# One comparison a chunk pair with a product in its other arm; 1/rms and gates inside the selections; the last scatter prepared ahead of the last products

## The chip, the core and the metric

The kernel runs on one core of a Trainium2 chip. Time is device time in microseconds, the median of three runs. The profile is of one further execution of the same program. TensorE (PE in the rows, PEld its weight loads) multiplies matrices, VectorE (DVE), ScalarE (ACT) and GpSimd (POOL) work on elements, SyncE's queue (SPq) issues the transfers from the chip's memory.

## The reference

A decoder trunk of two layers over 256 tokens of 1024 channels, float32. The change lies in the second half of layer 1, an expert layer that sends each token to two of eight experts, and in the final norm:

```python
def moe_swiglu(h, router_w, wg, wu, wd):          # h: RMS-normed, D = 1024
    logits = (t @ router_w).astype(jnp.float32)
    top_val, top_idx = lax.top_k(logits, TOP_K)   # 2 of 8
    gates = jax.nn.softmax(top_val, axis=-1)
    combine = jnp.sum(jax.nn.one_hot(top_idx, N_EXPERTS, dtype=jnp.float32) * gates[..., None], axis=1)
    for e in range(N_EXPERTS):                    # EXPERT_DIM = 3584
        he = jax.nn.silu(t @ wg[e]) * (t @ wu[e])
        out = out + (combine[:, e:e + 1].astype(t.dtype) * he) @ wd[e]
```

Around it, `h = h + moe_swiglu(rms_norm(h, ln_ffn_odd), ...)` and at the end `rms_norm(h, final_g)`. Ahead of it stand layer 0 (attention, a recurrent block, a dense SwiGLU) and the pooling mixer of layer 1; the change leaves them as they are.

## The kernel before

The order of the instructions on each engine is written out by hand; semaphores between engines are set by the framework.

**Routing.** Behind the pooling mixer `h` is complete (`band_out`, L819). It is transposed into `hT` (L844 to L850), multiplied with the router weights (`logits`, L830), and VectorE ranks the eight logits of each token (L858 to L864). Three small products give each token its slot in each expert's list (L866 to L870; `pos` L895, `cnt` L896: how many tokens an expert has). Short products on constants (`keep_warm`, L89) run in between. The squares of `h` (`squares`, L239, on ScalarE) and the nine steps of 1/rms (`finish_rs`, L223 to L243, on VectorE) come beside and behind this. Two banks of results, `go` and `yo`, are set to zero by products with a zeroed tile (L914 to L916).

**Slots.** An expert has room for 96 slots, 64 main ones (C0) and 32 more (C1). `gather_a` (L929) compares slot numbers with `pos` and so makes the selection, four comparisons an expert; `gather_b` (L939) multiplies `h` with it and `gather_c` (L944) applies the norm's gain and stores the expert's tokens in `xe`. Four small products (`slot_scales`, L955) give each slot its 1/rms and its gate; a copy (L957) keeps them.

**Chunks.** Each of the 8 experts is cut into 7 chunks of 512 hidden channels, 56 in all. A chunk has four gate/up pieces and two down pieces of 1 MB, loaded on SyncE's queue in the order: gate/up of chunk n, then down of chunk n-1. The stage has about twenty buffers for them, reused in a fixed turn; a buffer's next load is issued when the products that read it are done (`finished`, `load_free`, L144). Per chunk, TensorE does: `gate_up_main` (L971), 64 slots, two products side by side; then, only where the expert has more than 64 tokens, `gate_up_more` (L983), 32 products of 32 columns, four side by side, inside a branch (L978); ScalarE and VectorE then form silu(gate) x up with the slot scales (`hidden_a`, L990 and L991), while TensorE does `down_main` of the chunk before (L1008) and, in a second branch (L1014), its `down_more` (L1019, 8 products); last, three transposes (L997) whose result ScalarE copies (L999) for the next chunk's down products. A branch is TensorE's alone: its sequencer compares a register that holds whether the expert is full. In a full expert both branches run their products, in a small one they are skipped.

Jobs between the quarters of `gate_up_main` are listed by chunk and quarter (`do(n, q, ...)`, run by `due`): the next expert's selection and gather in the last four chunks of an expert, its slot scales in the last one, and the finished expert's scatter in the next expert's second and third chunk: `scatter_a` (L1031, L1032) transposes the selection, `scatter_b` (L1041) multiplies it with the results that `results` copied from `y` and `yo` (L1023, L1024), `scatter_c` (L1049) adds onto `ho`.

**End.** Behind the last chunk come, in this order, the last down products, `results`, `scatter_a`, and twice `scatter_b` with `scatter_c`; then `norm_out`: the final gains are spread over the partitions by four products (L1068) and copied (L1069), squares of `ho` (L239), the nine steps, four scalings (L1156) and four output transfers (L1157). A block for experts with more than 96 tokens stands behind a branch at the end and is not run with these inputs.

Of the kernel before, what the change touches and what calls it, by code (L numbers as in the profile page):

```python
# [18 lines left out]
P = 128  # L19
S = 256  # L20
# [37 lines left out]
def hybrid_kernel(ctx, tc, x, cst, prm, row, gate, rtr, w_in, w_out, w_gu, w_dn, w_pool, m_gu, m_dn, out):  # L58
# [613 lines left out]
    sc2 = late.tile([P, NT, E, 2], F32, name="sc2")  # L672
# [168 lines left out]
    for t in range(NT):  # L841
        band_out(t, 0)
    tb = [transpose_pair(kk) for kk in range(2)]
# [6 lines left out]
    dve.tensor_copy(hT[:, 6:8, :], tb[1])  # L850
    lgb = bank("tp", "lg")
# [4 lines left out]
    squares(0)  # L856
# [17 lines left out]
    squares(1)  # L874
# [34 lines left out]
    sel, xe, scl, het, y_ = {}, {}, {}, {}, {}  # L909
    yt = late.tile([P, W], F32, tag="band", name="yt")  # L910
    ysb, selT = yt[:, 0:1024].rearrange("p (a c) -> p a c", a=2), yt[:, 1024:1536].rearrange("p (a s) -> p a s", a=2)

    go, yo = bank2("go", "go"), bank2("yo", "yo")
    pool.memset(ysb, 0.0)  # L914
    for b in (go, yo):
        pe.matmul(b, ysb[:, 0, 0:P], ysb[:, 0], start=True, stop=True)  # L916

    def counted():
        dve.tensor_reduce(gt[:, 2, 0:1], cnt, axis=AX.X, op=OP.max)
        dve.tensor_copy(most, gt[:, 2, 0:1])  # L920
# [26 lines left out]
    def each_slot(s_):  # L947
        return s_.rearrange("p t m s -> p t (m s)")[:, :, P - C0:P + C1]
# [16 lines left out]
    def gate_up_main(n, b, i):  # L965

        x_ = xe[n // EP % 2]
        for kk in range(2):
            for c in range(2):
                k = 2 * i + kk  # L970
                pe.matmul(b[c * C0:(c + 1) * C0], x_[:, k, 0:C0], block(MOE[n] + i, (2 * kk + c) * 512), start=k == 0, stop=k == KD - 1)  # L971
# [3 lines left out]
    def gate_up_more(n):  # L975

        x_ = xe[n // EP % 2]
        with tc.If(big[n // EP] > 0, preferred_fallthrough_block=True):  # L978
            for k in range(KD):
                for c in range(2):  # L980
                    for r in range(2):
                        q = (2 * c + r) * C1
                        pe.matmul(go[q:q + C1, 0:2 * P], x_[:, k, C0:CAP], block(MOE[n] + k // 2, (k % 2 * 2 + c) * 512 + r * 2 * P, 2 * P),  # L983
                                  start=k == 0, stop=k == KD - 1)
# [344 lines left out]
```

## Time and profile before

| | us |
|---|---|
| median of three runs | 1201.91 (1201.18 to 1203.38) |
| the profiled execution | 1200.26 |
| its span, first to last instruction | 1198.5 |
| TensorE busy in the span | 1144.6 (96%) |
| VectorE, ScalarE, GpSimd busy | 300.1, 255.1, 99.5 |
| mean granted clock of TensorE | 0.988 |

The span is that of the profiled execution alone, so sums from its rows are made against 1200.26. A row of the timeline begins with the start in us from the span's first instruction and the time of the merged instructions; in square brackets stands the idle time ahead of it and what ended it. PEq is TensorE's sequencer. A product in float32 is recorded as two instructions, and the ends of products are modelled, so products that follow each other overlap in the rows: the time from one to the next is read from their starts.

### The profile page before, as it was taken

How to read it: one execution, taken by the hardware profiler on the slowest of the kernel's cores; microseconds unless marked ns; L12 is line 12 of the kernel's file. 1: busy time of each engine (PE TensorE's matmuls, PEld its weight loads, DVE VectorE, ACT ScalarE, POOL GpSimd, SP SyncE). 2: the span in 40 equal slices, each digit the busy share in tenths (PEclk: the TensorE clock that was granted, in tenths of full speed). 3: DMA queues.
4: the chain of work that ended last, by engine and by line, in shares of the span. 5: the costliest groups of instructions: out<-in, count | busy, mean ns of one | idle time of the engine just before them, and what ended most of it. 6: DMA issues, size and time to landing. Idle time of an engine off the chain costs nothing. (4 is left out here: it accounts for less than half of the span.)

```text
span 1198.5 us, 17142 instructions
## 1 busy us (share of the span) xinstructions
PE 1144.6 (96%) x7098; PEld 593.3 (50%) x7099; DVE 300.1 (25%) x566; ACT 255.1 (21%) x489; POOL 99.5 (8%) x115
## 2 busy tenths in 40 slices
PE   7989999999999999998989999999999999999994
PEld 6877999999843433332323443333334333443331
DVE  6686665455720011011001000200110010001002
ACT  5855544444500010110000000100100000001011
POOL 3723151112100000000000000000000000000000
PEclk8989999999999999999999999999999999999998
DMA  9444955555599999999999999999999999999951
GB/s 350 142 141 162 363 188 181 206 177 205 214 381 415 419 415 419 415 415 418 416 419 414 417 415 414 421 401 418 415 403 416 415 419 415 380 362 390 407 222 38
DMA packets 69633, 408.70 MB, mean 341 GB/s; under 512 B 7828, under 2 KB 8088, under 8 KB 31128
## 3 DMA queue, kind: packets, MB, share of 16 engines
q1 hardware_dynamic: 69384, 407.08, 85.0%
q8 instruction: 81, 1.33, 0.4%
q10 hardware_dynamic: 144, 0.10, 0.1%
q14 instruction: 24, 0.20, 0.0%
HBM read 406.10 MB, written 1.05 MB: 340 GB/s over the span
## 5 line engine op out<-in xcount | busy, mean ns | idle before, releaser
L971 PE MATMUL mg<-raw,xe 128*64 128x512 f32 x920 | 211.2, 598 | 4.2 <-DMA raw<-in_m_gu 4.0
L991 DVE SCALAR_TENSOR_TENSOR sg<-sg,scl,mg 128x256 f32<-128x256 f32 x56 | 26.9, 480 | 396.2 <-ACT sg L990 396.2
L168 DVE TENSOR_TENSOR lo<-raw,hi 128x1024 fp32r<-128x1024 f32 x80 | 100.0, 1270 | 95.7 <-ACT hi L167 95.5
L971 PEld LDWEIGHTS mg<-raw,xe 128*64 128x64 f32 x920 | 61.2, 136 | 121.8 <-issue 104.8
L990 ACT ACTIVATE sg<-mg,scl 128x256 f32<-128x256 f32 x56 | 26.6, 475 | 439.4 <-PE mg L971 439.4
L1008 PE MATMUL y<-raw,het 128*64 128x512 f32 x440 | 101.9, 598 | 7.4 <-PEq L978 4.5
L167 ACT ACTIVATE hi<-raw 128x1024 fp32r<-128x1024 f32 x96 | 98.7, 1052 | 43.3 <-PE dn L185 28.3
L999 ACT COPY het<-tp 128x384 f32<-128x384 f32 x56 | 26.8, 479 | 232.1 <-PE tp L997 231.7
L1008 PEld LDWEIGHTS y<-raw,het 128*64 128x64 f32 x440 | 32.3, 136 | 71.1 <-issue 63.7
L1008 PE MATMUL y<-twohi,het 128*64 128x512 f32 x116 | 53.6, 598 | 3.7 <-PEq L978 3.1
L971 PE MATMUL mg<-twohi,xe 128*64 128x512 f32 x212 | 55.8, 605 | 0.0
L971 PE MATMUL mg<-twolo,xe 128*64 128x512 f32 x212 | 54.5, 592 | 0.0
L1008 PE MATMUL y<-twolo,het 128*64 128x512 f32 x116 | 53.6, 600 | 0.2 <-DMA twolo<-in_m_dn 0.2
L185 PE MATMUL gu<-xfl,hi 128*128 128x256 f32 x352 | 50.3, 283 | 0.0
L185 PE MATMUL gu<-xfh,hi 128*128 128x256 f32 x352 | 50.1, 283 | 0.0
L185 PE MATMUL gu<-xfh,lo 128*128 128x256 f32 x352 | 50.0, 283 | 0.0
L185 PEld LDWEIGHTS gu<-xfh,hi 128*128 128x128 f32 x352 | 46.3, 191 | 0.9
L185 PEld LDWEIGHTS gu<-xfl,hi 128*128 128x128 f32 x352 | 45.7, 192 | 0.2 <-DVE xfl L270 0.2
L185 PEld LDWEIGHTS gu<-xfh,lo 128*128 128x128 f32 x352 | 45.7, 192 | 0.0
L168 POOL TENSOR_TENSOR lo<-raw,hi 128x1024 fp32r<-128x1024 f32 x16 | 39.3, 2456 | 70.8 <-ACT hi L167 54.0
L997 PEld LDWEIGHTS tp<-pr,sg 128*128 128x128 f32 x168 | 17.4, 140 | 53.8 <-issue 51.7
L971 PE MATMUL mg<-spare,xe 128*64 128x512 f32 x176 | 42.0, 598 | 0.0
(384 smaller groups left out, 1410.8 us busy)
## 6 DMA issues: line engine op xcount, KB each, us to landing
raw<-in_m_gu SPq DMA_DIRECT2D x115, 1024.0 KB, 16.0
raw<-in_m_dn SPq DMA_DIRECT2D x55, 1024.0 KB, 17.3
twohi<-in_m_gu SPq DMA_DIRECT2D x53, 512.0 KB, 12.3
twolo<-in_m_gu SPq DMA_DIRECT2D x53, 512.0 KB, 12.5
raw<-in_w_gu SPq DMA_DIRECT2D x22, 1024.0 KB, 4.9
spare<-in_m_gu SPq DMA_DIRECT2D x22, 1024.0 KB, 12.3
twohi<-in_m_dn SPq DMA_DIRECT2D x29, 512.0 KB, 13.1
twolo<-in_m_dn SPq DMA_DIRECT2D x29, 512.0 KB, 12.6
```

The source lines that it names most:

```text
L167: act.activation(hi, r, AF.Copy)
L168: eng.tensor_tensor(lo, r, hi.bitcast(F32), op=OP.subtract)
L185: pe.matmul(dst, l, r, start=start, stop=stop)
L971: pe.matmul(b[c * C0:(c + 1) * C0], x_[:, k, 0:C0], block(MOE[n] + i, (2 * kk + c) * 512), start=k == 0, stop=k == KD - 1)
L990: act.activation(v_, g_[:, :, 0, :], AF.Silu, scale=s4[:, a:a + 1])
L991: dve.scalar_tensor_tensor(v_, v_, s4[:, a + 1:a + 2], g_[:, :, 1, :], op0=OP.mult, op1=OP.mult)
L997: pe.transpose(b[:, i * P:(i + 1) * P], sg[:, i, :], ident)
L999: act.copy(het[n].rearrange("p a c -> p (a c)"), b[:, 0:3 * P])
L1008: pe.matmul(y_[e][j * C0:(j + 1) * C0], het[n][:, r, c * C0:(c + 1) * C0], block(DOWN[n] + c, (2 * j + r) * 512), start=p == c == r == 0, ...
```

## The change

The square sums of `h` move up between `band_out` and the logits, and 1/rms is finished before them. The two banks are zeroed by ScalarE. The gather's selection holds 1/rms (one comparison with a multiplication for each of the two token tiles), and a second selection, made by `gates` in each expert's fourth chunk, holds the gate and is transposed for the scatter in the fifth (`scatter_a`); `slot_scales` is gone, and `hidden_a` has no scales. Per chunk there is one branch (two in an expert's first chunk, one for each expert): its arm holds `gate_up_more` of this chunk and `down_more` of the one before, and its other arm one product of one column. The second of the eight k-products of `gate_up_main` (k = 1) is put behind the branch. The scatter multiplies the second part of the slots first. The gains of the final norm are made in the last chunk's second quarter; at the end, the two halves of the last scatter have banks of their own, and the squares go token tile by token tile. The block for more than 96 tokens is adapted alike.

```diff
...
     for t in range(NT):
         band_out(t, 0)
+    squares(0)
     tb = [transpose_pair(kk) for kk in range(2)]
...
     dve.tensor_copy(hT[:, 6:8, :], tb[1])
+    squares(1)
+    finish_rs()
     lgb = bank("tp", "lg")
     logits(lgb)
...
     keep_warm(WARM[0], ones)
-    squares(0)
...
-    squares(1)
 
     def slot_scalars_a():
...
     def slot_scalars_b():
         act.activation(gt[:, 1], gt[:, 0], AF.Tanh, scale=0.5)
 
-        one8 = cs[:, C_ONE:C_ONE + E]
-        for t in range(NT):
-            dve.tensor_scalar(sc2[:, t, :, 0], one8, rs[:, t:t + 1], None, op0=OP.mult)
         for t in range(NT):
             dve.scalar_tensor_tensor(cmb[:, t, :], sgn[:, t, :], gt[:, 1, t:t + 1], mskb[:, t, :], op0=OP.mult, op1=OP.add)
-        for t in range(NT):
-            dve.tensor_scalar(sc2[:, t, :, 1], cmb[:, t, :], rs[:, t:t + 1], 0.5, op0=OP.mult, op1=OP.mult)
+        dve.tensor_scalar(cmb, cmb, 0.5, None, op0=OP.mult)
...
+    selr = late.tile([P, NT, P], F32, name="selr")
+    selg = yt[:, 1536:2048].rearrange("p (t m s) -> p t m s", t=NT, m=2)
+
     go, yo = bank2("go", "go"), bank2("yo", "yo")
-    pool.memset(ysb, 0.0)
-    for b in (go, yo):
-        pe.matmul(b, ysb[:, 0, 0:P], ysb[:, 0], start=True, stop=True)
+    act.activation(go[:, 0:2 * P], iota.rearrange("p (o s) -> p o s", o=1).to_broadcast([P, 2, P]), AF.Copy, scale=0.0)
+    act.activation(yo, iota.rearrange("p (o s) -> p o s", o=1).to_broadcast([P, 4, P]), AF.Copy, scale=0.0)
...
     def gather_a(e):
-
-        s_ = sel[e] = (yt[:, 1536:2048].rearrange("p (t m s) -> p t m s", t=NT, m=2) if e % 2 else
-                       late.tile([P, NT, 2, P], F32, tag="sel", name="sel"))
+        for t in range(NT):
+            dve.tensor_scalar(selr[:, t, 0:CAP], iota[:, 0:CAP], pos[:, t, e:e + 1], rs[:, t:t + 1], op0=OP.is_equal, op1=OP.mult)
+
+    def gates(e):
         for t in range(NT):
             for m, (a, c) in enumerate(((0, C0), (C0, C1))):
-                dve.tensor_scalar(s_[:, t, m].rearrange("p (o s) -> p o s", s=c),
+                dve.tensor_scalar(selg[:, t, m].rearrange("p (o s) -> p o s", s=c),
                                   iota[:, a:a + c].rearrange("p (o s) -> p o s", o=1).to_broadcast([P, P // c, c]),
-                                  pos[:, t, e:e + 1], None, op0=OP.is_equal)
+                                  pos[:, t, e:e + 1], cmb[:, t, e:e + 1], op0=OP.is_equal, op1=OP.mult)
...
-    def slot_scales(e):
-
-        b = misc("sl")
-        for m in range(2):
-            for t in range(NT):
-                pe.matmul(b[:, 2 * m:2 * m + 2], sel[e][:, t, m], sc2[:, t, e, :], start=t == 0, stop=t == NT - 1)
-        scl[e] = work.tile([P, 4], F32, name="scl", bufs=2)
-        dve.tensor_copy(scl[e], b[:, 0:4])
...
-    def gate_up_main(n, b, i):
+    def gate_up_main(n, b, k):
 
         x_ = xe[n // EP % 2]
-        for kk in range(2):
+        for c in range(2):
+            pe.matmul(b[c * C0:(c + 1) * C0], x_[:, k, 0:C0], block(MOE[n] + k // 2, (k % 2 * 2 + c) * 512), start=k == 0, stop=k == 1)
...
-        with tc.If(big[n // EP] > 0, preferred_fallthrough_block=True):
-            for k in range(KD):
...
+    def more(parts):
+
+        for e in sorted({n // EP for _, n in parts}):
+            with tc.If(big[e] > 0, preferred_fallthrough_block=True) as c:
+                for f, n in parts:
+                    if n // EP == e:
+                        f(n)
+            with c.Else():
+                pe.matmul(go[0:C1, 511:512], idb[:, 0:C1], idb[:, 0:1], start=True, stop=True)
 
     def hidden_a(n, b):
-        s4 = scl[n // EP]
         sg = work.tile([P, 3, P], F32, name="sg", bufs=2)
-        for v_, g_, a in ((sg[:, 0:2], gates_of(b), 0), (sg[:, 2:3], gates_of(go[:, 0:2 * P]), 2)):
-            act.activation(v_, g_[:, :, 0, :], AF.Silu, scale=s4[:, a:a + 1])
-            dve.scalar_tensor_tensor(v_, v_, s4[:, a + 1:a + 2], g_[:, :, 1, :], op0=OP.mult, op1=OP.mult)
+        for v_, g_ in ((sg[:, 0:2], gates_of(b)), (sg[:, 2:3], gates_of(go[:, 0:2 * P]))):
+            act.activation(v_, g_[:, :, 0, :], AF.Silu)
+            dve.tensor_tensor(v_, v_, g_[:, :, 1, :], op=OP.mult)
         return sg
...
     def results(e):
+        dve.tensor_copy(ysb[:, 1], yo)
         act.copy(ysb[:, 0], y_[e])
-        dve.tensor_copy(ysb[:, 1], yo)
...
-    def scatter_b(t, n=2):
-        bs = [misc(f"sc{t}{j}") for j in range(2)]
-        for m in range(n):
+    def scatter_b(t, room=lambda name: misc(name)):
+        bs = [room(f"sc{t}{j}") for j in range(2)]
+        for m in (1, 0):
             for j in range(2):
-                pe.matmul(bs[j], selT[j * C0:(j + 1) * C0, m, t * P:(t + 1) * P], ysb[j * C0:(j + 1) * C0, m], start=m == 0, stop=m == n - 1)
+                pe.matmul(bs[j], selT[j * C0:(j + 1) * C0, m, t * P:(t + 1) * P], ysb[j * C0:(j + 1) * C0, m], start=m == 1, stop=m == 0)
         return bs
...
+    def late_gains():
+        fg[0] = raws.tile([P, W], F32, tag="raw", name="fg")
+        for j in range(2):
+            final_gain(j)
...
-    do(0, 3, slot_scales, 0)
     do(0, 4, load_big, 0)
-    for e in range(1, E):
+    for e in range(E):
         n = e * EP
...
+        if e:
+            do(n - 4, 2, gather_a, e)
+            do(n - 3, 1, gather_next, e, 0)
+            do(n - 3, 3, gathered, e, 0)
+            do(n - 2, 1, gather_next, e, 1)
+            do(n - 2, 3, gathered, e, 1)
+            do(n, 1, load_big, e)
+            do(n + 1, 1, scatter_next, 0)
+            do(n + 1, 3, scattered, e - 1, 0)
+            do(n + 2, 1, scatter_next, 1)
+            do(n + 2, 3, scattered, e - 1, 1)
+        do(n + 3, 0, gates, e)
+        do(n + 4, 1, scatter_a)
+    do(N - 1, 1, late_gains)
...
     for n in range(N):
         b = bank2("gu", f"mg{n}", 2)
-        for i in range(4):
-            due(n, i)
-            gate_up_main(n, b, i)
+        for k in range(KD):
+            if k % 2 == 0:
+                due(n, k // 2)
+            if k != 1:
+                gate_up_main(n, b, k)
         due(n, 4)
-        gate_up_more(n)
+        more([(gate_up_more, n)] + [(down_more, n - 1)] * (n > 0))
+        gate_up_main(n, b, 1)
         for i in range(4):
             finished(MOE[n] + i)
         sg = hidden_a(n, b)
         if n:
             for c in range(2):
                 down_main(n - 1, c)
-            down_more(n - 1)
...
+    more([(down_more, N - 1)])
     for c in range(2):
         down_main(N - 1, c)
-    down_more(N - 1)
...
         o = raws.tile([P, W], F32, tag="raw", name="out").rearrange("p (t d) -> p t d", t=NT)
-        fg[0] = raws.tile([P, W], F32, tag="raw", name="fg")
         js = [slice(j * 512, (j + 1) * 512) for j in range(2)]
-        for j in range(2):
-            final_gain(j)
-        for j in range(2):
-            squares(j, src=ho[0])
+        for t in range(NT):
+            for j in range(2):
+                squares(j, (t,), src=ho[0])
...
     results(E - 1)
-    scatter_a(sel[E - 1])
+    bs = [scatter_b(0), scatter_b(1, lambda name: bank2("gu", name, 2))]
     for t in range(NT):
-        scatter_c(t, scatter_b(t))
+        scatter_c(t, bs[t])
     norm_out()
...
```

## Rows read from the trace of the kernel before

**Rows 1.** TensorE's waits, 549-621.3 and 621.3-1170 us: total, times, longest.

```profile
PE mg L971 <- DMA raw<-in_m_gu: 4.0, 8, 0.6
...
PE y L1008 <- PEq L978: 4.4, 14, 0.4
```

**Rows 2.** The timeline of TensorE, at chunks 21 and 35.

```profile
621.20 1.94 PE L971 MATMUL mg<-raw,xe 128*64 128x512 f32 x8 [0.56 <-DMA raw<-in_m_gu]
...
838.55 1.89 PE L971 MATMUL mg<-sparel,xe 128*64 128x512 f32 x8
```

**Rows 3.** Sums by stretches: length, busy (five engines), clock, DMA share, GB/s.

```profile
621.20:838.50 217.30, 213.98 (x1394) 80.44 (x1396) 23.00 (x54) 18.91 (x44) 0.00 (x0) 1.00 1.01 415
...
1020.00:1110.00 90.00, 89.23 (x636) 33.99 (x629) 8.26 (x18) 7.35 (x17) 0.00 (x0) 1.00 0.96 376
```

**Rows 4.** The page's DMA queues: packets, MB.

```profile
DMA packets 69633, 408.70 MB, mean 341 GB/s; under 512 B 7828, under 2 KB 8088, under 8 KB 31128
...
q1 hardware_dynamic: 69384, 407.08, 85.0%
```

**Rows 5.** Sums by stretches, at the stage's start.

```profile
343.00:346.00 3.00, 1.91 (x11) 0.73 (x11) 0.74 (x2) 1.21 (x3) 0.00 (x0) 1.00 0.53 150
```

**Rows 6.** The timeline at the stage's start: VectorE, TensorE, SyncE's queue.

```profile
326.89 0.17 DVE L858 COPY rt__1143<-lg 128x16 f32<-128x16 f32 x1 [2.90 <-PE lg L830]
...
329.69 1.18 PE L916 MATMUL go<-yt 128*128 128x512 f32 x2
...
331.57 3.71 PE L939 MATMUL xe<-sel,h 128*128 128x96 f32 x32
...
343.56 0.80 SPq L144 DMA_DIRECT2D raw<-in_m_dn  x2
```

**Rows 7.** The timeline of TensorE in small and full chunks.

```profile
467.47 3.65 PE L1008 MATMUL y<-raw,het 128*64 128x512 f32 x16 [0.31 <-PEq L978]
...
471.27 0.52 PE L997 MATMUL tp<-pr,sg 128*128 128x128 f32 x3
...
501.10 1.05 PE L955 MATMUL sl<-sc,sel 128*128 128x2 f32 x8
...
630.91 0.60 PE L1031 MATMUL st<-pr,sel 128*128 128x128 f32 x4
...
679.23 3.65 PE L1008 MATMUL y<-raw,het 128*64 128x512 f32 x16
...
682.81 1.92 PE L1019 MATMUL yo<-raw,het 128*32 128x512 f32 x16
```

**Rows 8.** The timeline of the tail, all engines.

```profile
1173.96 0.59 PE L1008 MATMUL y<-twohi,het 128*64 128x512 f32 x1
...
1174.39 0.59 PE L1008 MATMUL y<-twohi,het 128*64 128x512 f32 x1
...
1175.04 0.59 ACT L1023 COPY yt<-y 128x512 f32<-128x512 f32 x1 [3.75 <-PE y L1008]
...
1181.40 1.28 DVE L1049 TENSOR_TENSOR ho<-ho,sc 128x512 f32<-128x512 f32 x2 [1.47 <-PE sc L1041]
1182.14 1.99 PE L1068 MATMUL fg<-fr,pr 4*128 4x256 f32 x8 [0.18 <-DVE ho L1049]
...
1184.65 0.63 ACT L239 ACTIVATE junk<-ho 128x512 bf16<-128x512 f32 x1
...
1187.66 0.16 DVE L243 SCALAR_TENSOR_TENSOR nwt<-ssq 128x2 f32<-128x2 f32 x1 [4.98 <-ACT junk L239]
```

**Rows 9.** The page's costliest groups: busy, mean ns of one.

```profile
L991 DVE SCALAR_TENSOR_TENSOR sg<-sg,scl,mg 128x256 f32<-128x256 f32 x56 | 26.9, 480 | 396.2 <-ACT sg L990 396.2
...
L990 ACT ACTIVATE sg<-mg,scl 128x256 f32<-128x256 f32 x56 | 26.6, 475 | 439.4 <-PE mg L971 439.4
```

**Rows 10.** Sums by stretches, TensorE alone: length, busy, clock, DMA share, GB/s.

```profile
327.00:328.00 1.00, 1.00 (x7) 0.50 0.96 377
```

**Rows 11.** TensorE's sequencer, L978: ns min/median/max, first and last start.

```profile
L978 PEldq COMPARE_BRANCH  x77: 65/179/436, 341.7 to 1161.6; - x77
```

More of the change, by code (lines that the diff above doesn't have):

```diff
@@ L977, in gate_up_more @@
         x_ = xe[n // EP % 2]
-        with tc.If(big[n // EP] > 0, preferred_fallthrough_block=True):
-            for k in range(KD):
[L980 to L984, printed above, removed]
+        for k in range(KD):
+            for c in range(2):
+                for r in range(2):
+                    q = (2 * c + r) * C1
+                    pe.matmul(go[q:q + C1, 0:2 * P], x_[:, k, C0:CAP], block(MOE[n] + k // 2, (k % 2 * 2 + c) * 512 + r * 2 * P, 2 * P),
+                              start=k == 0, stop=k == KD - 1)
+    def more(parts):
[6 more added lines that the diff above has]
+                pe.matmul(go[0:C1, 511:512], idb[:, 0:C1], idb[:, 0:1], start=True, stop=True)
     def hidden_a(n, b):
-        s4 = scl[n // EP]
         sg = work.tile([P, 3, P], F32, name="sg", bufs=2)
-        for v_, g_, a in ((sg[:, 0:2], gates_of(b), 0), (sg[:, 2:3], gates_of(go[:, 0:2 * P]), 2)):
-            act.activation(v_, g_[:, :, 0, :], AF.Silu, scale=s4[:, a:a + 1])
-            dve.scalar_tensor_tensor(v_, v_, s4[:, a + 1:a + 2], g_[:, :, 1, :], op0=OP.mult, op1=OP.mult)
+        for v_, g_ in ((sg[:, 0:2], gates_of(b)), (sg[:, 2:3], gates_of(go[:, 0:2 * P]))):
+            act.activation(v_, g_[:, :, 0, :], AF.Silu)
+            dve.tensor_tensor(v_, v_, g_[:, :, 1, :], op=OP.mult)
         return sg
@@ L1013, in down_more, with scatter_a @@
         e, p = divmod(n, EP)
-        with tc.If(big[e] > 0, preferred_fallthrough_block=True):
-            for r in range(2):
-                for j in range(2):
-                    for c in range(2):
-                        q = (2 * j + c) * C1
-                        pe.matmul(yo[q:q + C1], het[n][:, 2, (2 * c + r) * C1:(2 * c + r + 1) * C1], block(DOWN[n] + c, (2 * j + r) * 512),
-                                  start=p == r == 0, stop=p == EP - 1 and r == 1)
+        for r in range(2):
+            for j in range(2):
+                for c in range(2):
+                    q = (2 * j + c) * C1
+                    pe.matmul(yo[q:q + C1], het[n][:, 2, (2 * c + r) * C1:(2 * c + r + 1) * C1], block(DOWN[n] + c, (2 * j + r) * 512),
+                              start=p == r == 0, stop=p == EP - 1 and r == 1)
     def results(e):
+        dve.tensor_copy(ysb[:, 1], yo)
         act.copy(ysb[:, 0], y_[e])
-        dve.tensor_copy(ysb[:, 1], yo)
-    def scatter_a(s_):
+    def scatter_a():
         b = misc("st")
@@ L1069, in final_gain @@
         act.copy(fg[0][:, j * 512:(j + 1) * 512], b)
-    bs = [gather_b(each_slot(sel[0]), k4) for k4 in range(2)]
+    bs = [gather_b(selr[:, :, 0:CAP], k4) for k4 in range(2)]
     for k4 in range(2):
@@ L1120, in hybrid_kernel @@
         b = bank2("gu", f"mg{n}", 2)
-        for i in range(4):
-            due(n, i)
-            gate_up_main(n, b, i)
+        for k in range(KD):
+            if k % 2 == 0:
+                due(n, k // 2)
+            if k != 1:
+                gate_up_main(n, b, k)
         due(n, 4)
-        gate_up_more(n)
+        more([(gate_up_more, n)] + [(down_more, n - 1)] * (n > 0))
+        gate_up_main(n, b, 1)
         for i in range(4):
@@ L1139, in hybrid_kernel @@
             sp.dma_start(fr[0:4], row[:, R_FG:R_FG + D].rearrange("o (j c) -> (o j) c", j=4))
+    more([(down_more, N - 1)])
     for c in range(2):
         down_main(N - 1, c)
[L1142 removed]
     def norm_out():
         o = raws.tile([P, W], F32, tag="raw", name="out").rearrange("p (t d) -> p t d", t=NT)
[L1147 removed]
         js = [slice(j * 512, (j + 1) * 512) for j in range(2)]
[L1149 to L1152 removed]
+        for t in range(NT):
+            for j in range(2):
+                squares(j, (t,), src=ho[0])
         finish_rs()
@@ L1171, in rest_of @@
     def rest_of(e, r):
-        s_ = late.tile([P, NT, 2, P], F32, tag="sel", name="sel2").rearrange("p t m s -> p m t s")[:, 0]
-        s2 = work.tile([P, NT, 2], F32, name="s2", bufs=1)
+        s_ = selr
         x_ = rawb.tile([P, W], F32, tag="raw", name="x_")[:, 0:D].rearrange("p (k s) -> p k s", k=KD)
@@ L1178, in rest_of @@
             dve.tensor_scalar(s_[:, t, :], iota, pos[:, t, bass.ds(e, 1)], -float(CAP + r * P), op0=OP.subtract, op1=OP.is_equal)
-            dve.tensor_copy(s2[:, t, :], sc2[:, t, bass.ds(e, 1), :])
+            dve.tensor_scalar(selg[:, t, 0], s_[:, t, :], cmb[:, t, bass.ds(e, 1)], None, op0=OP.mult)
+            dve.tensor_scalar(s_[:, t, :], s_[:, t, :], rs1[:, t:t + 1], None, op0=OP.mult)
         for k4 in range(2):
             gather_c(x_, k4, gather_b(s_, k4))
-        b = misc("so")
-        for t in range(NT):
-            pe.matmul(b[:, 0:2], s_[:, t, :], s2[:, t, :], start=t == 0, stop=t == NT - 1)
-        s4 = work.tile([P, 4], F32, tag="scl", name="s4", bufs=2)
-        dve.tensor_copy(s4[:, 0:2], b[:, 0:2])
         b = misc("to")
         for t in range(NT):
-            pe.transpose(b[:, t * P:(t + 1) * P], s_[:, t, :], ident)
+            pe.transpose(b[:, t * P:(t + 1) * P], selg[:, t, 0], ident)
         dve.tensor_copy(selT[:, 0], b[:, 0:S])
```

37 lines of the change are left out of this document (10 added, 27 removed).

## The prediction

> **What bounds the kernel now.** I read the waits of TensorE by stretches first, then its timeline where they end, then the sums by stretches, and last the tail. The expert stage has 56 chunks of 6 weight pieces (4 gate/up, 2 down). From 549 to 621 us TensorE waits again and again for a landing piece, eight times for gate/up pieces alone [rows 1], and the last such gap stands ahead of 621.20, the fourth piece of chunk 21 [rows 2]: up to there the weights set the pace. From there on TensorE does: its main wait left is not for data but for its own sequencer at the branch of L978, 14 times 0.3 us [rows 1], in the 14 small chunks behind that point, and it is busy for 213.98 of 217.30 us from 621.2 to 838.5 [rows 3]. Late in the stage the loads wait for it: 376 GB/s from 1020 to 1110 us [rows 3]. So time taken out of TensorE ahead of 621 us is worth nothing by itself; taken out behind, it reaches the end, but only so far as the weights are there in time; and the tail behind the last product counts in full.
>
> How much may be taken out before the weights bind again: between the fourth piece of chunk 21 (621.20) and that of chunk 35 (838.55) [rows 2] lie 84 pieces of 1.0486 MB, 88.1 MB. The 415 GB/s of [rows 3] count all queues; q1 has 407.08 of 408.70 MB [rows 4], so 413.4 GB/s are weights, and 88.1 MB take 213.1 us of the 217.3. TensorE can gain 4.2 us there and no more. Behind chunk 35 stand two full experts (14 chunks) and a small one; the loads that wait from 1020 us on show that the stock of pieces grows there, and nothing clips.
>
> **The change part by part.**
>
> *Start of the stage.* At 343 to 346 us the load queue ran dry: 150 GB/s instead of 415 [rows 5], which loses 3 x (1 - 150/415) = 1.9 us; the next loads are issued at 343.56, when chunk 0 frees its pieces [rows 6]. As the weights set the pace up to 621 us, these 1.9 us reach the end. The change takes out the two zero products of L916 (329.69 up to the gather at 331.57, 1.9 us) and the slot scales of chunk 0 (1.0 us, below), so the pieces come free some 2.9 us sooner, about when the queue runs dry: gain 1.9 us. The square sums and the nine short steps for 1/rms move ahead of the logits; VectorE stood idle for 2.90 us before it took the logits [rows 6], and ScalarE zeroes the two banks with nothing else to do. If this cover fails, the steps delay the gather and the gain falls to nothing; bounds 0 and 2.3.
>
> *Slot scales.* Four products an expert disappear, 1.05 us busy [rows 7], of which the last 0.05 overlap: 1.0 us. For experts 4 and 5 they lie between chunks 21 and 35 (2.0 us), for 6 and 7 behind (2.0 us). The scaling moves into the comparisons (two for the gather, four for the gates) and out of L990 and L991, on engines that have room; nothing on the path.
>
> *One branch a chunk with a product in its other arm.* In a small chunk TensorE stands for 0.31 us at L978, and from the end of y at 467.47 + 3.65 to 471.27, for 0.15 us, at L1014 [rows 7]. It lets its products run dry before its sequencer makes up the count of those left out. With a product in that arm the count can ride on it, so I take both waits as gone, less 0.15 us for the product and its change of tile width: 0.3 us a small chunk, bounds 0 and 0.46. In a full chunk the 8 pairs of y take 3.58 us up to the start of yo [rows 7], against 8 x 0.43 at the pitch of y in [rows 8]: 0.14 us for a change of width. The new order has one change fewer: 0.14 us a full chunk, bounds -0.15 (a jump over the other arm) and 0.3. The Trainium skill, "TensorE: Matmul & The Clock Gate", section Part 3: Packing small matmuls, says that matmuls end in the order of the program, so that one count on the last is sound. By this the run-dry is unneeded and both waits go; where the count is still made up by a wait, the sum is that of rival A.
>
> The product k = 1 now comes behind the branch and ahead of ScalarE's gate function, so the chain L990 to L991 (475 and 480 ns, and a smaller pair beside it) [rows 9] begins later against the transposes that wait for it; the down products of 3.65 us still lie between and cover it. At the last place where a weight piece is awaited (chunk 35) its two pairs, 0.86 us, slip from before the wait to behind it: a loss of 0.86. The full arm's down products come ahead of y, whose pieces follow those of gate/up in the queue; they are behind a branch in which 3.4 us of gate/up work stand first.
>
> So between chunks 21 and 35: 2.0 + 7 small x 0.3 + 7 full x 0.14 = 5.1 us, clipped to 4.2. Behind: 2.0 + 7 x 0.3 + 14 x 0.14 - 0.86 = 5.2 us.
>
> *Moved into the last expert.* The transposes for expert 7's scatter (0.60 us at 630.91, some 0.5 up to the next product [rows 7]) and the gains (1.99 us at 1182.14 [rows 8]) now run between products while TensorE is the bound: -2.5 us, so 2.7 us remain. They issue no DMA; ScalarE's two gain copies stand ahead of the last gate function and are done long before it.
>
> *Tail.* Count from the last down product, 1174.39 [rows 8]. Before: copy at +0.65, transposes and selection copy, scatter products and adds of one half and then of the other (its adds at +7.01), gains, squares at +10.26, 1/rms at +13.27. After: the second-arm results are copied during the last products, their scatter products run during ScalarE's copy (+0.65 to +1.24), the others from +1.3 to +2.4 (two pairs, 0.43 apart, 0.6 long); two adds, 1.28, to +3.7; the second half has banks of its own, products to +4.15, adds to +5.5; the squares (3.01 us for four, 0.75 each) follow each add, the last from +5.6 to +6.4. Gain 13.27 - 6.4 = 6.9 us; bounds 5 and 7.5. The nine steps, four outputs and their transfers behind stay.
>
> Sum: 1.9 + 4.2 + 2.7 + 6.9 = 15.7 us. The profiled execution took 1200.26 us (span 1198.5 and 1.8 around it), so 1184.6; the median of the runs shown is 1.65 us above it, so I predict 1186.2.
>
> **Rivals.**
> A. The other arm still runs dry before it counts. Then its product adds what the second branch saves, and only slot scales and full chunks gain: 1.9 + 3.0 + 0.6 + 6.9 = 12.4, 1189.5 us. For it: every small chunk does so now [rows 1]. Against: that arm holds no product yet to count on.
> B. The start gains nothing, as the gather waits for 1/rms or the clock stays low: 1188.1 us. For it: the granted clock was 0.50 at 327 us (1.2 of 2.4 GHz), after the narrow logit products [rows 10], and the change removes two wide products that followed. Against: the gather takes their place at once.
> C. The tail keeps an order that I do not see (the result copies in series, all scatter products behind both): 3.5 instead of 6.9, 1189.6 us.
> D. Slower: the branch itself grows. The true arm now holds 40 products, so every jump over it reaches farther, and every full chunk jumps over the other arm. If the target's code must be fetched first, all 35 chunks behind 621 us pay. From 15.7/35 = 0.45 us net a chunk the gain is gone; at 1 us it is 1186.2 + 35 = 1221 us. Against: over a skip of 32 products the branches of L978 took 65 to 436 ns [rows 11]. The Trainium skill, "Runtime: NRT & Kernel Launch", section Instruction fetch mechanics, states that a taken branch whose target lies outside the loaded window stalls for a fetch; no row here shows such a stall.
>
> **How the numbers follow.** Chances: forecast 0.57, A 0.21, B 0.10, C 0.07, D 0.05. The upper bounds (2.3, 4.2, 5, 7.5) give 19, or 1183; the lower (0, 2.0, 0, 5) give 7, or 1195. A, B and C lie inside, D is left out; with 1.5 us below for the spread of runs the range is 1181.5 to 1195. A measurement of this kernel tells 0.2% (2.4 us) from no change. All cases but D are faster by more: faster 0.92; 0.03 for no change, where A, B and C meet with some unseen loss; 0.05 slower.
>
> **What would show it.** No dry spell of loads near 343 us; the last landing wait of TensorE near 836, not 621 us, at chunk 34 or 35; no wait of y on TensorE's sequencer; no sl products; 6.4 us from the last down product to the first step of 1/rms. Waits at the branch that stay speak for A; gaps at the branch above 0.4 us, in full chunks too, for D. The forecast is wrong if the weights bind far beyond chunk 35, so that loop savings vanish, or if the tail is above 9 us.

## The result and the profile after

The changed kernel takes 1183.66 us (median of four, 1182.78 to 1185.29) against 1201.55 for the kernel before on the same chip (four, 1201.12 to 1203.38): a ratio of 0.9851, 95% interval 0.9836 to 0.9866. The forecast was 1186.2 with a range of 1181.5 to 1195.0. All medians here are of fast runs; one slow run of e11, an experiment below (1435.39 us at a granted clock of 0.748) is in none of them. The profiled executions took 1200.26 and 1183.04 us (spans 1198.5 and 1181.3); the 17.2 us between them are split here at five places that both traces have:

| from, to | before | after | gained | forecast |
|---|---|---|---|---|
| start, piece 4 of chunk 21 | 621.20 | 620.50 | 0.70 | 1.9 |
| to piece 4 of chunk 35 | 217.35 | 212.99 | 4.36 | 4.2 |
| to the last down product | 335.84 | 331.65 | 4.19 | 2.7 |
| to the first step of 1/rms | 13.27 | 6.55 | 6.72 | 6.9 |
| to the end of the span | 10.82 | 9.58 | 1.24 | 0 |

TensorE's waits after the change, in the stretches that answer to [rows 1] (total, times, longest), first 549 to 620.5 us (four smaller ones of y are left out):

```profile
PE mg L957 <- DMA raw<-in_m_gu: 6.8, 10, 1.4
PE mg L957 <- DMA spare<-in_m_gu: 1.6, 1, 1.6
...
```

and 620.5 to 1160 us, in which these two are all there is:

```profile
PE mg L957 <- DMA raw<-in_m_gu: 1.8, 3, 0.7
PE mg L957 <- DMA sparel<-in_m_gu: 0.6, 1, 0.6
```

The wait of y on TensorE's sequencer, 14 times in [rows 1], is gone, and some waits for weights have come behind 620.5. The timeline of TensorE says where, at the places of [rows 2]:

```profile
620.50 1.94 PE L957 MATMUL mg<-raw,xe 128*64 128x512 f32 x8 [0.56 <-DMA raw<-in_m_gu]
...
828.50 1.94 PE L957 MATMUL mg<-raw,xe 128*64 128x512 f32 x8 [0.69 <-DMA raw<-in_m_gu]
830.99 1.94 PE L957 MATMUL mg<-raw,xe 128*64 128x512 f32 x8 [0.56 <-DMA raw<-in_m_gu]
833.49 1.94 PE L957 MATMUL mg<-sparel,xe 128*64 128x512 f32 x8 [0.56 <-DMA sparel<-in_m_gu]
```

Three pieces of chunk 35 are waited for, where before none was. TensorE has caught up with the load queue there, which is the clip of the forecast. The sums by stretches, against [rows 3] and [rows 5] (length, busy of five engines, clock, DMA share, GB/s), show the queue still at its 415 GB/s, and the dry spell at the start mostly filled:

```profile
343.00:346.00 3.00, 2.06 (x11) 0.82 (x11) 0.62 (x2) 1.03 (x3) 0.00 (x0) 1.00 0.99 344
620.50:833.50 213.00, 211.21 (x1388) 78.05 (x1388) 21.64 (x56) 15.48 (x44) 0.00 (x0) 1.00 1.01 416
1020.00:1110.00 90.00, 90.00 (x605) 33.94 (x605) 8.07 (x18) 6.13 (x17) 0.00 (x0) 1.00 0.97 389
```

A small chunk in TensorE's timeline (against 467.47 and 471.27 in [rows 7]): the other arm's product stands 0.11 us before the next product, and nothing waits at the branch. From the start of y to that of the transposes it is 3.53 us, where it was 3.80.

```profile
1143.10 0.18 PE L979 MATMUL go<-idb 128*32 128x1 bf16 x1
...
1143.21 1.08 PE L957 MATMUL mg<-raw,xe 128*64 128x512 f32 x4
...
1144.12 3.60 PE L1002 MATMUL y<-raw,het 128*64 128x512 f32 x16
1147.65 0.55 PE L991 MATMUL tp<-pr,sg 128*128 128x128 f32 x3
```

The stage's start, against [rows 6], timeline of all engines, and under it TensorE's sums by stretches (length, busy, clock, DMA share, GB/s). The gather begins 1.5 us earlier and takes 6.04 us where it took 3.71; the granted clock is 0.50 (1.2 of 2.4 GHz) from 328.0 to 334.8, for 4.7 of these 6.04 us. Before, it was 0.50 from 326.5 to 329.9, and the gather began behind that.

```profile
330.08 6.04 PE L939 MATMUL xe<-selr,h 128*128 128x96 f32 x32
...
336.05 6.23 PE L957 MATMUL mg<-raw,xe 128*64 128x512 f32 x28
...
342.42 1.35 SPq L144 DMA_DIRECT2D raw<-in_m_dn  x2
```

```profile
326.00:328.00 2.00, 2.00 (x20) 0.99 0.98 410
328.00:330.00 2.00, 1.38 (x11) 0.50 1.02 418
330.00:332.00 2.00, 1.94 (x10) 0.50 0.98 297
332.00:334.00 2.00, 2.00 (x11) 0.50 0.99 385
334.00:336.00 2.00, 2.00 (x16) 0.80 1.04 418
```

The tail, against [rows 8]: copy, adds of either half, last square, first step of 1/rms.

```profile
1165.14 0.59 PE L1002 MATMUL y<-twolo,het 128*64 128x512 f32 x1
...
1165.78 0.59 ACT L1017 COPY yt<-y 128x512 f32<-128x512 f32 x1 [3.75 <-PE y L1002]
...
1167.68 1.28 DVE L1042 TENSOR_TENSOR ho<-ho,sc 128x512 f32<-128x512 f32 x2 [5.39 <-PE sc L1034]
...
1169.40 1.28 DVE L1042 TENSOR_TENSOR ho<-ho,sc 128x512 f32<-128x512 f32 x2 [0.43 <-PE sc L1034]
...
1170.93 0.63 ACT L239 ACTIVATE junk<-ho 128x512 bf16<-128x512 f32 x1
...
1171.69 0.16 DVE L243 SCALAR_TENSOR_TENSOR nwt<-ssq 128x2 f32<-128x2 f32 x1 [1.01 <-ACT junk L239]
```

### The profile page after: what moved, and what is told of

Same layout as the page of the kernel before. It is cut to its first block, busy times and chain, and to the rows that moved or that the text cites. A ratio compares the mean times of both kernels' runs of the same rounds, so it can differ in the third digit from the quotient of the medians.

```text
span 1181.3 us, 16799 instructions
## 1 busy us (share of the span) xinstructions
PE 1136.6 (96%) x7071; PEld 584.0 (49%) x7071; DVE 294.3 (25%) x572; ACT 243.0 (21%) x491; POOL 98.5 (8%) x114
## 3 DMA queue, kind: packets, MB, share of 16 engines
HBM read 406.10 MB, written 1.05 MB: 345 GB/s over the span
## 4 chain that ended last, share of the span: by engine, by line
PE 66%; DMA 25%; DVE 4%; ACT 3%; issue 1%; SPq 0%; DVEq 0%; ACTq 0%
PE mg L957 21%; PE gu L185 11%; PE y L1002 10%; DMA raw<-in_m_gu 7%; PE go L968 6%; PE dn L185 5%; DMA raw<-in_m_dn 4%; PE yo L1012 3%; DMA spare<-in_m_gu 3%; DMA twohi<-in_m_gu 3%; DMA twolo<-in_m_gu 2%; PE sc L1034 2%; DMA sparel<-in_m_gu 2%; DMA spareh<-in_m_gu 2%; PE xe L939 2%; DMA sparehl<-in_m_dn 1%
## 5 line engine op out<-in xcount | busy, mean ns | idle before, releaser
L957 PE MATMUL mg<-raw,xe 128*64 128x512 f32 x920 | 217.7, 601 | 10.8 <-DMA raw<-in_m_gu 10.5
L985 DVE TENSOR_TENSOR sg<-sg,mg 128x256 f32<-128x256 f32 x56 | 23.6, 421 | 574.2 <-ACT sg L984 574.2
L984 ACT ACTIVATE sg<-mg 128x256 f32<-128x256 f32 x56 | 21.5, 384 | 569.1 <-PE mg L957 569.1
L957 PEld LDWEIGHTS mg<-raw,xe 128*64 128x64 f32 x920 | 58.4, 136 | 125.7 <-issue 95.0
L968 PE MATMUL go<-raw,xe 128*32 128x256 f32 x704 | 41.3, 380 | 0.0
## 6 DMA issues: line engine op xcount, KB each, us to landing
spare<-in_m_gu SPq DMA_DIRECT2D x22, 1024.0 KB, 11.5
```

What stands on the lines that cost most here:

```text
L984: act.activation(v_, g_[:, :, 0, :], AF.Silu)
L985: dve.tensor_tensor(v_, v_, g_[:, :, 1, :], op=OP.mult)
```

## The experiments

Each is an edit of the changed kernel unless it says otherwise. The kernel before took 1202.0 to 1202.1 us beside them. "Small" and "full" are the pitch of a small and a full chunk (before 11.65 and 16.52, after 11.19 and 16.39), "closing" the time from the first step of the last 1/rms to the end of the span, all from the one profiled execution of each. By the times only e4 is clear of the changed kernel (0.9836 to 0.9866): the intervals of all other edits of it overlap that one, so there the sizes are read from the profiles.

| | median us | ratio, 95% interval | small | full | closing |
|---|---|---|---|---|---|
| e1, no other arm | 1185.38 | 0.9855, 0.9840 to 0.9871 | 11.31 | 16.39 | 9.49 |
| e2, two branches | 1186.14 | 0.9870, 0.9855 to 0.9885 | 11.29 | 16.52 | 9.63 |
| e3, k in order | 1183.04 | 0.9841, 0.9827 to 0.9854 | 11.19 | 16.39 | 9.47 |
| e4, gains early | 1180.25 | 0.9820, 0.9806 to 0.9833 | 11.19 | 16.39 | 8.89 |
| e5, old tail | 1186.24 | 0.9872, 0.9857 to 0.9887 | | | 9.58 |
| e6, zero products | 1183.79 | 0.9849, 0.9836 to 0.9863 | | | 9.47 |
| e7, 12 warming products | 1182.26 | 0.9841, 0.9828 to 0.9855 | | | 9.45 |
| e8, e3 and e4 | 1181.76 | 0.9833, 0.9820 to 0.9847 | 11.19 | 16.39 | 10.83 |
| e10, e8 with 5 loads | 1182.69 | 0.9837, 0.9825 to 0.9850 | 11.19 | 16.39 | 11.00 |
| e11, e3 with 4 loads | 1183.91 | 0.9842, 0.9829 to 0.9854 | 11.19 | 16.39 | 10.68 |
| e12, before with 5 loads | 1204.11 | 1.0012, 1.0003 to 1.0021 | 11.65 | 16.52 | 11.07 |

### What the branch is worth

**e1.** The product in the other arm is left out.

```diff
-            with c.Else():
-                pe.matmul(go[0:C1, 511:512], idb[:, 0:C1], idb[:, 0:1], start=True, stop=True)
```

> The changed kernel without the product in the branch's other arm (the one branch a chunk stays). Theory (the product carries the count, so TensorE needn't run dry): the run-dry comes back, y or k=1 waits 0.3 us for TensorE's sequencer in each small chunk, a small chunk without jobs takes 11.5 to 11.65 us instead of 11.19. Between chunks 21 and 35 the 7 x 0.35 = 2.4 us eat the 1.8 us of waits for pieces at chunk 35 and cost 0.6; in the last expert 7 x 0.35 = 2.4 come through: 3 us slower than the changed kernel's 1183.7, near 1186.7. Rival (the merging of two branches is what gained): small chunks stay at 11.2 and the time stays within 1 us of 1183.7.

TensorE waits for its sequencer at the branch again, here behind 846 us, in the seven small chunks of the last expert (total, times, longest):

```profile
PE mg L957 <- PEq L974: 1.1, 7, 0.2
```

A small chunk takes 11.31 us, 0.12 more than after the change and 0.34 less than before; the theory's 11.5 to 11.65 was missed. The run-dry is back, but it is not that of before. Before, a small chunk waited at two branches, 0.31 us at the first; here it waits at one, for 0.16 us. Merging took one of the two waits away with its branch, and about half of the other; why that one got shorter is open. In the median the step is 1.7 us, of the 3 that were expected, and not clear of the spread.

**e2.** Two branches as before, each with the product in its other arm: `down_more` gets its own `more(...)` behind `down_main`.

```diff
-        more([(gate_up_more, n)] + [(down_more, n - 1)] * (n > 0))
+        more([(gate_up_more, n)])
...
                 down_main(n - 1, c)
+            more([(down_more, n - 1)])
```

> The changed kernel with two branches a chunk again, each with its product in the other arm; the second one stands behind the down products, as in the kernel before. Theory (the product gained, the merging little): small chunks 11.19 + 0.15 = 11.35 us, full ones 16.39 + 0.13 = 16.52; between chunks 21 and 35 the 2 us are taken by the waits for pieces there, behind them 14 x 0.13 + 7 x 0.15 = 2.9 us come through: 1186.5. Rival (the merging gained half or more of the 0.46 us a small chunk): small chunks 11.4 or longer and 1187.5 or more.

Small 11.29, full 16.52. So one branch without the arm's product saves 0.34 us a small chunk, the products without the merging 0.36, both together 0.46. These don't add, as both act on the same two waits: the merging leaves one wait of 0.16 us, the products leave none, but cost 0.11 us each, and here a chunk has two of them. The 0.13 of a full chunk are the merging alone; whether the branch or the change of width is what it saves, no run takes apart.

### Where k = 1 belongs

**e3.** All eight products of `gate_up_main` in order, ahead of the branch.

```diff
...
-            if k != 1:
-                gate_up_main(n, b, k)
+            gate_up_main(n, b, k)
...
-        gate_up_main(n, b, 1)
```

> The changed kernel with all eight gate/up products in order ahead of the branch. Theory (putting k=1 behind the branch only slips 0.86 us from before the wait for the last piece of chunk 35 to behind it): the stretch from that piece to the last down product is 0.9 us shorter than 331.6, 1182.8 in all. Rival (the product behind the branch covers something, the start of the gate function or the sequencer's branch): small or full chunks grow by 0.1 us or more and the time is 1184 to 1188.

TensorE's timeline at the last awaited piece:

```profile
832.93 1.94 PE L957 MATMUL mg<-sparel,xe 128*64 128x512 f32 x8 [0.55 <-DMA sparel<-in_m_gu]
834.80 0.18 PE L979 MATMUL go<-idb 128*32 128x1 bf16 x1
```

From there to the last down product it is 330.80 us, against 331.65: 0.85 less, the 0.86 that the forecast had charged for the slip. The small chunk stays at 11.19, so the position behind the branch buys nothing by the chunk. In the time the gain doesn't stand out from the spread (1181.07 to 1183.58, five runs). The low clock at the start lasts 3.4 us in this profile and not 6.8; the part on the start comes back to that.

### Gains and tail

**e4.** The gains of the final norm are made in chunk 17 instead of the last one; one of the piece buffers is given up for them, at its first release from chunk 12 on.

```diff
...
-        fg[0] = raws.tile([P, W], F32, tag="raw", name="fg")
...
-    do(N - 1, 1, late_gains)
+    do(17, 1, late_gains)
...
+        if i >= MOE[12] and (taken, i) in slots:
+            slots.remove((taken, i))
+            fg[0] = late.tile([P, W], F32, tag="hl", name="fg")
```

> The changed kernel with the final gains made in chunk 17, where the weights set the pace, instead of in the last chunk; they take one of the stage's twenty piece buffers from about chunk 14 on. Theory (work is free where TensorE waits for pieces, and costs in full in the last chunk): the last chunk is 2.07 us shorter, nothing else moves: 1181.6. Rival 1 (the missing buffer starves TensorE): longer waits for pieces at chunks 14 to 21 and 35, 1184 or more. Rival 2 (the gains in the last chunk were hidden): no change.

The best time of all, with five runs from 1179.69 to 1180.95. The last down product comes 2.05 us earlier (1163.09), about the 1.99 that the gains take in [rows 8]; chunk 17 lies where weights are awaited, so there they cost nothing: piece 4 of chunk 21 comes at 620.43, for 620.50. Another 0.69 us of the step lies in the closing stretch (9.58 to 8.89), behind all that the edit moves. The spread shrinks too: the changed kernel's runs lie 2.5 us apart, these 1.3. What may add to that spread is in the profile of e1, which still has the gains in the last chunk. TensorE's timeline, then its sums by stretches:

```profile
1152.21 2.00 PE L1058 MATMUL fg<-fr,pr 4*128 4x256 f32 x8
1154.14 4.43 PE L957 MATMUL mg<-raw,xe 128*64 128x512 f32 x12
```

```profile
1152.00:1154.00 2.00, 2.00 (x10) 1.00 0.00 0
1154.00:1156.00 2.00, 2.00 (x7) 0.52 0.00 0
1156.00:1158.00 2.00, 2.00 (x10) 0.63 0.00 0
```

Right behind the gains, products of four rows, the granted clock is at the lower of its levels for 3.4 us, and the chunk takes 15.03 us, against 13.26 in the changed kernel's profile. It is in this one of the seven profiles that have the gains in the last chunk.

**e5.** The tail's end as before: gains behind the scatter, squares half by half, both halves of the scatter in the same banks. The transposes stay in the loop.

```diff
-    do(N - 1, 1, late_gains)
...
-        for t in range(NT):
-            for j in range(2):
-                squares(j, (t,), src=ho[0])
+        late_gains()
+        for j in range(2):
+            squares(j, src=ho[0])
...
-    bs = [scatter_b(0), scatter_b(1, lambda name: bank2("gu", name, 2))]
     for t in range(NT):
-        scatter_c(t, bs[t])
+        scatter_c(t, scatter_b(t))
...
```

> The changed kernel with the end as it was: the gains behind the last chunk, the squares behind both halves, the second half of the last scatter in the banks of the first (the scatter's transposes stay early). Theory (the terms add up): from the last down product to the first step of 1/rms 11.5 to 12 us instead of 6.55; the last chunk 2.07 us shorter; 3 us slower than the changed kernel, 1186.8. Rival (the narrow gain products in the last chunk also lower TensorE's clock in some executions, and cost up to 1.7 us more there): 1185 to 1186.

From the last down product to 1/rms it is 11.57 us, against 6.55; the product itself comes 2.08 us earlier, since the gains left the chunk. Net 2.95 in the span, 2.6 in the median. The second half of the scatter waits for the adds of the first, as all engines' timeline says:

```profile
1165.60 1.28 DVE L1042 TENSOR_TENSOR ho<-ho,sc 128x512 f32<-128x512 f32 x2 [5.39 <-PE sc L1034]
...
1166.35 2.58 PE L1034 MATMUL sc<-yt 64*128 64x512 f32 x8 [0.77 <-DVE ho L1042]
```

### The stage's start

**e6.** The banks are zeroed by two wide products again.

```diff
-    act.activation(go[:, 0:2 * P], iota.rearrange("p (o s) -> p o s", o=1).to_broadcast([P, 2, P]), AF.Copy, scale=0.0)
-    act.activation(yo, iota.rearrange("p (o s) -> p o s", o=1).to_broadcast([P, 4, P]), AF.Copy, scale=0.0)
+    pool.memset(ysb, 0.0)
+    for b in (go, yo):
+        pe.matmul(b, ysb[:, 0, 0:P], ysb[:, 0], start=True, stop=True)
```

> The changed kernel with the two banks zeroed by products again, as in the kernel before, instead of by ScalarE. Theory (without these wide products the clock stays at 1.2 GHz for 6.8 instead of 3.4 us and the first gather takes 6 instead of 3.7): the low stretch is 3.4 us, the gather 3.7; as the products themselves take 1.9 us, chunk 0 begins within 0.5 us of the changed kernel's 336.05, and the time is within 1 us of 1183.7. Rival (the length of the low stretch hangs on where it falls against the logits and the idle time behind them, not on these products): 6.8 us here too, chunk 0 begins near 338, 1185 to 1186.

The stretch at 1.2 GHz is 6.8 us long here too (328.2 to 335.0), so it isn't the missing products that lengthen it. The first load comes 2.0 us later (344.42), piece 4 of chunk 21 by 0.96 (621.46); the median is that of the changed kernel, within its spread. That is the time of the theory, but not by its way.

**e7.** Twelve short products on constants instead of eight run ahead of the slot numbers.

```diff
-WARM = (8, 4, 8)
+WARM = (12, 4, 8)
```

> The changed kernel with 12 instead of 8 warming products behind the logits: they fill the 0.62 us for which TensorE stands idle before the position products. Theory (that idle time keeps the clock at 1.2 GHz through the first gather): low stretch 3.4 us, gather 3.7, chunk 0 begins near 334.3, the first loads are issued 1 to 1.5 us earlier and so does everything up to chunk 35: 1182.5. Rival (filling it doesn't bring the clock back): low stretch 6.8, at the lower clock the four products delay the positions: 1183.7 to 1184.7.

The slow stretch keeps its 6.8 us and begins earlier (325.3); piece 4 of chunk 21 comes 1.23 us earlier (619.27), the median 1.4. The theory's 3.4 us did not come, though its time did; that the products act on the clock is not shown. What sets the length of that stretch stays open: it is 3.4 us in the profiles of before, e3 and e10, 6.8 in after, e1, e2, e4 to e7 and e12, 10.2 in e8, e9 and e11. It is not the instructions up to there alone: the loads that e10 to e12 add stand behind chunk 7, long after it, and yet it is 3.4 in e10 for 10.2 in e8, 10.2 in e11 for 3.4 in e3, and 6.8 in e12 for 3.4 before.

### Both, and what the closing stretch does

**e8.** The edits of e3 and e4 together.

> The two experiments that gained, together: all eight gate/up products in order, and the gains in chunk 17. Theory (0.85 us from the first, whatever the second gives, as they lie in different chunks): 1180.25 - 0.85 = 1179.4. Rival (they share the waits at chunk 35): 1180.3.

Missed by 2.4 us. Up to 1/rms the step is 0.60 us earlier than in e4 (1169.04 against 1169.64), though the clock was low for 10.2 us at the start; behind it the closing stretch takes 10.83 us, against 8.89. SyncE's queue, waits of its last instructions, in e4 and then in e8 (total, times, longest):

```profile
SPq L1220 <- SPq L1220: 0.7, 2, 0.5
```

```profile
SPq L1218 <- SPq L1218: 2.5, 2, 2.1
```

These are the two gaps right behind SyncE's closing branch, the jump over the block for more than 96 tokens. The kernel before has 2.5, 2, 2.0 there, the changed one 1.3, 2, 0.7. That gives the 1.24 us that the forecast lacks a place; e9 to e12 ask what it hangs on. e10 to e12 are padded in this way:

```diff
             sp.dma_start(fr[0:4], row[:, R_FG:R_FG + D].rearrange("o (j c) -> (o j) c", j=4))
+            for i in range(1, 6):
+                sp.dma_start(fr[4 * i:4 * i + 4], row[:, R_FG:R_FG + D].rearrange("o (j c) -> (o j) c", j=4))
```

**e9.** e8 once more, unchanged.

> The kernel of the last run once more, for one profile. From the first step of the last 1/rms to the end it took 10.83 us, against 8.88 with the early gains alone, and 2.05 of it lie between the two semaphore instructions that SyncE's queue executes behind its closing branch. Theory: the gap belongs to the program, namely to where that branch's target lies in SyncE's instructions (the kernel before, with as many instructions executed ahead of the branch, 925, has a gap of 1.94 at the same place, the eight kernels with 766 to 920 have none above 0.65, which is the landing of the last output): 10.8 again, gap 2.0. Rival: it belongs to the execution (a landing that came late): 8.9, no gap.

The gap is there again, 2.27 us; the one run took 1182.07. So it came in both profiles of this program, which speaks for the program and against chance.

**e10.** e8 with five such loads.

> The same kernel with five further loads of 4 KB on SyncE's queue behind chunk 7, into partitions that nothing reads: only the place of what follows in SyncE's instructions is changed (930 ahead of the branch). Theory: the gap of 2 us behind the closing branch goes or gets smaller, the closing stretch is 8.9 to 9.5 and the time 1180.2 to 1180.8 against 1181.76. Rival (the gap belongs to the execution, or to the order of the weight products): 10.8 or 8.9 by chance, time within 0.5 of 1181.8.

Missed: it stays (2.30 us). With 931 instructions executed up to the branch instead of 925 it is where it was, and the time is no better.

**e11.** e3 with four such loads (`range(1, 5)`).

> The kernel with k = 1 in its order (closing stretch 9.47 us, 1183.04 us) with four such loads, so that 925 instructions stand ahead of the closing branch, as in the two kernels that have the gap. Theory, if the count of instructions decides: closing stretch 10.8 us and the time 1184.4. Rival (count is chance): 9.5 and 1183.0. A weaker form of the theory (the place decides, but not by this count alone) allows both here and is decided by the other two.

The gap comes: 1.92 us behind the branch, one semaphore later, and the closing stretch goes from 9.47 to 10.68. SyncE's last waits in e3 and in e11:

```profile
SPq L1215 <- SPq L1215: 1.2, 2, 0.6
```

```profile
SPq L1217 <- SPq L1217: 2.4, 2, 1.9
```

The median is 0.9 us higher, which is inside the spread; the gap itself is in the profile.

**e12.** The kernel before with five such loads.

> The kernel before with five such loads behind chunk 7: its closing stretch of 10.82 us has a gap of 1.94 us at the same place, 1.3 us more than the landing of the last output asks for. Theory: the gap goes, the closing stretch is 9.5 us and the time 1.3 us under that of the kernel before, so that 1.3 us of the change's gain come from where code lies and not from what it does. Rival: the closing stretch stays at 10.8 and the time is that of the kernel before.

Missed: the gap stays (2.16 us), and the kernel is 2.0 us slower by the medians. Its piece 4 of chunk 21 comes at 625.26, 4.1 us late, 1.3 of it from the first load, with the low clock at the start 3.4 us longer than before; what the rest is, no run shows.

Together: the gap is in all six profiles with 925 to 931 instructions executed up to the branch (before, e8 to e12), and in none of the eight with 766 to 920, and four loads whose data nobody reads brought it. That fits a gap that hangs on where SyncE's instructions lie. It is argued and not shown: the loads add transfers to the queue as well as instructions, and no run parts the two. That the kernel before could lose the gap was not shown, as the padding tried there left it. The Trainium skill, "Runtime: NRT & Kernel Launch", section Instruction fetch mechanics, says that a taken branch whose target isn't in the loaded window stalls for a fetch. The gap behind this taken branch agrees with it in kind; that it is such a fetch no run here shows, since a packet on an instruction queue starts some 1.05 us behind the branch in e8 and in e3 alike.

## Why the prediction was right, and where it wasn't

The time came out 2.5 us under the forecast and inside its range; the mechanisms were those of the forecast in every large term, and the sizes of several were off. That the total lies so near has luck in it: of the rows, the start gave 1.2 us less than forecast and the closing stretch, of which the forecast says nothing, 1.24 more, and the stretch behind chunk 35 gave 1.5 more. With the other two rows that is 1.5 of the 2.5 us; the other 1.0 is that the forecast put the median 1.65 us above the profiled execution, where it is 0.62.

*Where time counts.* Right. Ahead of chunk 21 nothing but the earlier first load reached the end; between chunks 21 and 35 the gain stopped at 4.36 us, for 4.2 that 84 pieces at 413 GB/s allow; and the last wait for a piece is that of chunk 35 at 833.49, for about 836.

*Start.* Mis-sized: 0.70 for 1.9 us. The step that failed is that the pieces come free 2.9 us sooner. They came 1.14 sooner (343.56 to 342.42). 1.49 us were won up to the gather, and the gather then lost 2.33 at 1.2 GHz. By the same count as in the forecast the dry spell still costs 3 x (1 - 344/415) = 0.5 us; 0.4 more went between the first load and chunk 21; where, is not shown. This is the half of rival B that speaks of the clock, as a price of one term. Its reason, the two wide products taken out, fell with e6. How much it costs differs from profile to profile: in e3, which has the same instructions up to chunk 0, the low clock lasts 3.4 us as before, the gather takes 3.92, the first load is issued at 341.57, 2.0 us sooner than before, and piece 4 of chunk 21 comes 1.54 us sooner (619.66), near the 1.9.

*Slot scales.* 1.13 us an expert for 1.0: a small chunk with them took 12.78 against 11.65.

*The branch.* The product does what it was thought to: the waits are gone, and without it (e1) they come back. The gain is 0.46 us a small chunk, the upper bound, where 0.3 was taken. Two sizes made the difference. The wait at the second branch was read as 0.15 us from the end of y, and these ends are modelled; by the starts, from y to the transposes, 0.27 us went with it. At the first branch the forecast leaves 0.31 less 0.15 for the product and its change of width; the gate/up part is 0.22 shorter with the product in it, which moves the next one by 0.11. The transposes take 0.03 more. That merging alone (e1) keeps 0.34 of the 0.46 doesn't speak against the run-dry as the price: one wait went with its branch, and the other shrank. Full chunks gained 0.13, for 0.14. The Trainium skill, "TensorE: Matmul & The Clock Gate", section Part 3: Packing small matmuls, says that matmuls end in the order of the program. The trace agrees: in the changed kernel nothing waits for the sequencer behind a branch from 620.5 us on.

*k = 1.* Right: 0.86 us forecast as a loss, 0.85 measured by undoing it.

*Behind chunk 35.* 4.19 for 2.7. Most of the difference is the small chunks (7 x 0.16) and the slot scales (2 x 0.13). The rest is in the 2.5 us charged for what moved into the last expert. The gains cost 2.07 (a chunk of 13.26 for one of 11.19), but the transposes no 0.5: behind chunk 35 stand three sets of them in either kernel, before at 848, 974 and 1096 us (experts 4 to 6), after at 898, 1022 and 1126 (5 to 7), and these three cost 0.2 more. The one set that the loop has more stands ahead of chunk 21, where it costs nothing. With the measured sizes the same sum is 2 x 1.13 + 7 x 0.46 + 14 x 0.13 - 0.86 - 2.07 - 0.2 = 4.17. The bounds 0 and 5 that the forecast gives this stretch are not the sums of its parts' own bounds, which reach from -3.5 to 6.1.

*Tail.* 6.72 for 6.9, by its own steps: the copy at +0.64 (+0.65 was said), the second adds done at +5.5 (+5.5), the last square at +5.8 (+5.6), 1/rms at +6.55 (+6.4). e5 gives back 5.02 of it, with the old gains, squares and banks; the other 1.70 lies in what e5 keeps, the transposes moved ahead and the second part of the slots taken first, and no run takes these apart.

*The closing stretch.* Not in the forecast, which held that all behind 1/rms stays; this is a term that it put at nothing. It got 1.24 us shorter, and the place is a gap behind SyncE's last branch, 1.94 us before and 0.65 after. The changed kernel executes 777 instructions up to that branch, for 925; that this is why the gap went is not shown.

*Rivals.* A needs the waits at the branch to stay, C the order of copies and scatter of before, D gaps above 0.4 us; L974's comparisons take 65 to 421 ns, as in [rows 11], and the rows of the tail show the new order. None of the three came.

## What to carry to other kernels

Find the last place where the pacing resource is waited for, before and after: time taken out of the engine ahead of it is worth nothing, between the two it is clipped by the transfer's pace, behind them it counts in full; a product whose weights are there already (k = 1, in e3) belongs ahead of that place and not behind it. Narrow set-up products, such as the gains, go where the engine waits for weights (e4: 2.05 us up to the last down product), not into the last chunk. Read a wait from the starts of the products on either side where ends are modelled. Before a microsecond at the end of the trace is credited to an edit, look whether it lies in the queue that does nothing but wait.

## What was unexpected of the hardware

- With the two branches merged, the wait at the branch that was left fell too, from 0.31 us to 0.16 (e1). Why is open.
- The granted clock fell to 0.50 around the narrow products at the stage's start in every profile, for 3.4, 6.8 or 10.2 us, also where the instructions up to there are the same (e8 and e10, e3 and e11); and once, of seven profiles, behind eight products of four rows in the last chunk, for 3.4 us. The gather beside it took 3.71 to 6.83 us.
- A gap of 1.9 to 2.3 us behind the closing branch of a queue that has no more work came with four loads, five instructions, put far ahead of it (e3, e11); by what way is not shown.
